# Attention scores and the prompt's scores over all 128 rows of the matmul array, with zeros in the unused half

## The chip, the cores and the metric

One core of one Trainium2 chip. The metric is the device time of one launch in microseconds (us), the median of several runs. All inputs, weights and results are float32.

## What is computed

One inference step of a two-layer trunk over 640 tokens of 1024 features: 128 prompt tokens and 512 latent tokens. Each layer has a Fourier mixer beside differential attention (8 heads, two key maps of 64 features per head), sigmoid gates, an output projection and a gated feed-forward with a short convolution. The part that the change touches is the attention; latent queries see 128 cached keys and the 512 latent ones, prompt queries see the prompt only:

```python
def diff_attention(q, k, v, lam):
    ...
    scale = QK_DIM ** -0.5
    qb = jnp.moveaxis(q.reshape(b, nb, Q_BLOCK, N_HEADS, 2, QK_DIM), 1, 0)
    def one_block(qblk):
        s = jnp.einsum('bqhmd,bkhmd->bhmqk', qblk, k).astype(jnp.float32) * scale
        p = jax.nn.softmax(s, axis=-1)
        pd = p[:, :, 0] - lam * p[:, :, 1]
        return jnp.einsum('bhqk,bkhd->bqhd', pd.astype(v.dtype), v)
```

Here `m` runs over the two maps, `d` over the 64 features of one map, and a block is 128 queries.

## The kernel before

Activations lie transposed, features in partitions and the 640 tokens in columns, in 53 equal buffers of 640 columns ("slots") that are handed out in the order in which they were given back (`alloc`, `give`). A float32 operand that wants accuracy is split into a high part in the type float32r, which the array multiplies in one pass, and a low part, the rest, in the same type; a product is then high x high plus the two mixed ones. Every matmul of the program is issued in `mm` (L265), every transpose in `tr` (L268), so the profile shows these two lines for all of TensorE (PE), and rows are told apart by their tiles: `ps_d`, `ps_s` and `ps_t` are the accumulators (two buffers, one, one). Each matmul has a weight load of its own, in rows marked PEld.

Weights come as blocks of 1 MB into `w_raw` by DMAs that SP issues, are split into `w_h` (ACT L309, or POOL L311 outside attention) and `w_l` (DVE L315), and are used by the projections (`proj`, six matmuls of 320 columns per 128 features).

In attention the heads follow one another. `unit` makes four closures for a block of 128 queries: S0 and S1 (the scores of map 0 and map 1, each followed by its softmax), T (transposes of the combined probabilities), V (the product with the values). `layer` issues S0 of a block, a piece of projection work for the next head, T of the block before, a piece, S1, a piece, V of the block before, a piece. `FILL` sets how long the pieces are. The scheduler of the framework then orders each engine's queue. Per head there are four blocks of latent queries and one of the prompt, so 128 score maps of latent queries in the two layers.

A map of scores is computed in `s_map`. The queries' tile `S[m]` (from `q_epi`) holds the high part of map m's queries in that map's 64 partitions and the low part in the other 64. `KD[m]` (from `k_epi`) holds the high part of the keys in both halves, so that one matmul over 128 rows gives high x high plus low x high. The low part of the keys lies in `KL`, one tile for both maps, map 0 in partitions 0 to 63 and map 1 in 64 to 127; it is multiplied over 64 rows. For each of the two chunks of 320 keys:

```python
self.mm(out=o, lhsT=q, rhs=kd[:, ks], start=True, stop=False)
self.mm(out=o, lhsT=q[a:b], rhs=kl[a:b, ks], start=False, stop=True)
```

DVE then takes the maximum (L629), ACT the exponential (L631), and DVE combines the two maps (L640 to L643). The single `ps_s` is free for the next map when the exponential has read it. After V, ACT squares (L700), POOL makes the norm (L701, L702), DVE scales (L703), and the next T can reuse `ps_t`.

The prompt's scores are float32 products without a split: `qkp` holds its queries in columns 0 to 127 (L554) and its keys in 128 to 255 (L528), and each map takes 64 rows of it.

At the start of a layer the norm's output is made in `hn_one`: ACT L497, POOL L498 and DVE L499 for each of eight feature tiles, and the first projections take them one by one.

## Time and profile before

| what | value |
|---|---|
| runs | 2325.26, 2326.72, 2329.28 us, median 2326.72 |
| profiled execution | span 2324.8 us from the first to the last instruction; the page states no other time for it |
| PE | 2282.7 us busy, 98% of the span |
| weight loads (PEld) | 2122.7 us, 91% |
| DVE, ACT, POOL | 53%, 34%, 15% |
| granted TensorE clock, mean | 0.991 |

Engines are PE (TensorE's matmuls), PEld (its weight loads, which run beside the matmuls), DVE, ACT, POOL, and SP, which issues the DMAs. Matmuls are pipelined and their ends are modelled, so the start times of the weight loads are the better measure of how fast PE steps along. A bracket at the end of a row gives the idle time before it and what ended it; "issue" there means that the engine waited for nothing that the profile shows.

### The profile page before, as it was taken

To read this page: it belongs to the slowest core of one execution; us is meant where nothing else is said; L and a number is where in the kernel's file an instruction comes from. 1 tells how busy PE (TensorE), PEld (TensorE's weight loads), DVE (VectorE), ACT (ScalarE), POOL (GpSimd) and SP (SyncE) were. 2 spreads that over 40 slices of the span, in tenths; PEclk is the share of its full clock that TensorE was granted. 3 is DMA by queue.
4 is the path that set the end of the run, shared out by engine and by line. 5 is a ranking of instruction groups with operands and counts; after the bars stand their busy time and mean duration, and the time that the engine had idled before them with its cause. 6 is when DMAs were issued, how large, how long until landed. Compare 5 with 4: busy or idle time off the path is not lost.

```text
span 2324.8 us, 36711 instructions
## 1 busy us (share of the span) xinstructions
PE 2282.7 (98%) x15142; PEld 2122.7 (91%) x15142; DVE 1227.7 (53%) x2258; ACT 799.5 (34%) x1585; POOL 353.5 (15%) x550
## 2 busy tenths in 40 slices
PE   8999999999999999999999999999999999999998
PEld 5888888999999999999988888789999999999998
DVE  5665665324556553545466655752254565445454
ACT  4555554222133221313245555532122333122231
POOL 2111111101022000010051111210010410000001
PEclk8999999999999999999999999999999999999999
DMA  8222222222212332122212222222222122221221
GB/s 301 81 81 78 81 76 73 109 91 78 87 45 101 146 126 74 60 87 73 73 64 97 79 79 80 74 76 109 91 74 73 55 73 79 85 69 60 91 73 46
DMA packets 40631, 200.41 MB, mean 86 GB/s; under 512 B 4496, under 2 KB 12048, under 8 KB 19344
## 3 DMA queue, kind: packets, MB, share of 16 engines
q1 hardware_dynamic: 40464, 198.07, 24.5%
q8 instruction: 119, 1.95, 0.3%
q14 instruction: 48, 0.39, 0.1%
HBM read 193.33 MB, written 4.72 MB: 85 GB/s over the span
## 4 chain that ended last, share of the span: by engine, by line
PE 84%; issue 6%; DVE 4%; POOL 4%; ACT 2%; DMA 1%; POOLq 0%; SPq 0%; DVEq 0%; ACTq 0%
PE ps_d L265 48%; PE ps_s L265 19%; PE ps_t L265 15%; PE ps_t L268 2%; POOL slot L498 2%; POOL w_h L311 1%; ACT slot L497 1%; ACT slot L631 1%; POOL slot L515 0%; POOL ors L702 0%; ACT slot L534 0%; DVE slot L513 0%; DVE w_l L315 0%; PE ps_d L268 0%; DVE nm L629 0%
## 5 line engine op out<-in xcount | busy, mean ns | idle before, releaser
L265 PE MATMUL ps_d<-slot,w_h 128*128 128x320 f32 x5056 | 1000.0, 315 | 13.5 <-DVE slot L499 12.4
L265 PEld LDWEIGHTS ps_d<-slot,w_h 128*128 128x128 f32 x5056 | 796.0, 189 | 47.1 <-DVE slot L499 19.3
L265 PE MATMUL ps_d<-slot,w_l 128*128 128x320 f32 x2528 | 598.7, 311 | 2.6 <-DVE w_l L315 2.6
L315 DVE TENSOR_TENSOR w_l<-w_raw,w_h 128x512 fp32r<-128x512 f32 x520 | 362.6, 707 | 272.1 <-ACT w_h L309 158.5
L265 PEld LDWEIGHTS ps_d<-slot,w_l 128*128 128x128 f32 x2528 | 429.9, 189 | 3.4 <-DVE w_l L315 2.9
L309 ACT CAST w_h<-w_raw 128x512 fp32r<-128x512 f32 x308 | 188.4, 620 | 472.3 <-PE ps_d L265 244.3
L311 POOL TENSOR_SCALAR w_h<-w_raw 128x512 fp32r<-128x512 f32 x212 | 146.7, 693 | 1222.7 <-PE ps_d L265 622.2
L265 PE MATMUL ps_s<-slot,w_h 128*128 128x320 f32 x1376 | 264.8, 310 | 0.0
L265 PE MATMUL ps_t<-slot,w_h 128*128 128x320 f32 x1376 | 264.5, 309 | 0.0
L265 PEld LDWEIGHTS ps_t<-slot,w_h 128*128 128x128 f32 x1376 | 218.0, 188 | 1.7 <-issue 1.7
L265 PEld LDWEIGHTS ps_s<-slot,w_h 128*128 128x128 f32 x1376 | 217.8, 188 | 1.7 <-ACT slot L937 1.7
L631 ACT ACTIVATE slot<-ps_s,nm 128x640 f32<-128x640 f32 (+1 forms) x160 | 113.6, 710 | 187.1 <-DVE nm L629 184.0
L265 PE MATMUL ps_s<-slot,slot 128*128 128x320 f32 (+1 forms) x512 | 173.8, 392 | 0.9 <-ACT slot L631 0.2
L629 DVE TENSOR_REDUCE nm<-ps_s 128x1 f32<-128x640 f32 (+1 forms) x160 | 114.5, 716 | 104.2 <-PE ps_s L265 96.7
L265 PEld LDWEIGHTS ps_s<-slot,slot 128*128 128x128 f32 (+1 forms) x512 | 94.6, 185 | 78.7 <-issue 64.1
L265 PE MATMUL ps_t<-slot,w_l 128*128 128x320 f32 x688 | 164.6, 309 | 0.0
L265 PE MATMUL ps_s<-slot,w_l 128*128 128x320 f32 x688 | 164.6, 309 | 0.0
L932 DVE SCALAR_TENSOR_TENSOR slot<-ps_d,c_vecs,slot 128x511 f32<-128x511 f32 (+1 forms) x176 | 84.9, 543 | 64.5 <-ACT slot L937 64.5
L265 PEld LDWEIGHTS ps_s<-slot,w_l 128*128 128x128 f32 x688 | 117.1, 188 | 0.0
L265 PEld LDWEIGHTS ps_t<-slot,w_l 128*128 128x128 f32 x688 | 117.1, 188 | 0.0
L265 PE MATMUL ps_d<-w_h,slot 128*128 128x256 f32 x480 | 101.8, 293 | 0.6 <-DVE cols L427 0.6
L701 POOL TENSOR_SCALAR oms<-oss 128x1 f32<-128x1 f32 x80 | 24.7, 309 | 449.4 <-ACT junk L700 421.0
(164 smaller groups left out, 2254.2 us busy)
## 6 DMA issues: line engine op xcount, KB each, us to landing
w_raw<-in_w_stream SPq DMA_DIRECT2D x164, 1024.0 KB, 4.9
slot<-in_w_first SPq DMA_DIRECT2D x32, 256.0 KB, 5.6
w_raw<-in_w_stream SPq DMA_DIRECT2D x8, 768.0 KB, 4.3
slot<-in_x_t SPq DMA_DIRECT2D x8, 320.0 KB, 5.9
out_y_t<-slot SPq DMA_DIRECT2D x8, 320.0 KB, 2.2
c_big<-in_t_big SPq DMA_DIRECT2D x1, 1280.0 KB, 8.4
slot<-in_k_t SPq DMA_DIRECT2D x16, 64.0 KB, 1.8
slot<-in_v_h SPq DMA_DIRECT2D x16, 64.0 KB, 1.8
```

Source lines behind the costliest of these rows:

```text
L265: return self.nc.tensor.matmul(**a)
L268: return self.nc.tensor.transpose(*a)
L309: nc.scalar.copy(out=h[:, a:b], in_=raw[:, a:b])
L311: nc.gpsimd.tensor_scalar(out=h[:, a:b], in0=raw[:, a:b], scalar1=1.0, scalar2=0.0, op0=ALU.mult, op1=ALU.add)
L315: nc.vector.tensor_sub(out=lo[:, a:b], in0=raw[:, a:b], in1=h[:, a:b].bitcast(F32))
L497: nc.scalar.activation(out=H[:, a:b], in_=tmp[:, a:b], func=AF.Identity, scale=A, bias=B)
L498: (eng or nc.gpsimd).tensor_scalar(out=tmp[:, a:b], in0=tmp[:, a:b], scalar1=A, scalar2=B, op0=ALU.mult, op1=ALU.add)
L629: nc.vector.tensor_reduce(out=st["nm"][:, m:m + 1], in_=s_ap, axis=AX.X, op=ALU.max, negate=True)
L631: nc.scalar.activation(out=p[:, 0:n], in_=s_ap, func=AF.Exp, bias=st["nm"][:, m:m + 1], scale=1.0, accum_out=st["sum"][:, m:m + 1])
L701: nc.gpsimd.tensor_scalar(out=ms, in0=ss, scalar1=1.0 / 128, scalar2=EPS, op0=ALU.mult, op1=ALU.add)
L932: nc.vector.scalar_tensor_tensor(out=y[:, o0:o1], in0=ps[:, 192 + i0:192 + i1], scalar=w, in1=y[:, o0:o1], op0=ALU.mult, op1=ALU.add)
```

## The change

The low parts of the keys get a tile per map. `half_tiles` allocates two pairs of slots at the start of each layer (heads use them in turn) and clears the half that is never written; the pairs are given back when the layer's attention is over. The second matmul of each chunk then takes all 128 rows of the queries' tile and of the low keys, the other map's rows being multiplied by zeros. The prompt's queries go into one of two new constant tiles `pq`, map 0 in partitions 0 to 63 of its first 128 columns and map 1 in 64 to 127 of the second 128, with zeros elsewhere; it takes two ACT instructions in place of one, and the prompt's matmuls take 128 rows of it against the whole key tile `kp`. A setting of the launch makes room for the new tiles. The rest of the diff removes comments.

```diff
         self.gsub = [mk(f"c_gsub{l}", [128, 1]) for l in range(DEPTH)]
+        self.pq = [mk(f"c_pq{i}", [128, 256]) for i in range(2)]
...
-        hd = self.head[h] = dict(S=[self.alloc(F32R) for _ in range(2)], KD=[self.alloc(F32R) for _ in range(2)], KL=self.alloc(F32R),
-                                 pr=self.mid("qkp", 256))
+        hd = self.head[h] = dict(S=[self.alloc(F32R) for _ in range(2)], KD=[self.alloc(F32R) for _ in range(2)], KL=self.kl[h % 2],
+                                 pr=self.mid("kp"), pq=self.pq[h % 2])
...
-            nc.scalar.copy(out=hd["pr"][:, 128:256], in_=ps[:, 192:320])
-            nc.sync.dma_start(out=self.O["state_kt"][l, h], in_=hd["pr"][:, 128:256])
+            nc.scalar.copy(out=hd["pr"], in_=ps[:, 192:320])
+            nc.sync.dma_start(out=self.O["state_kt"][l, h], in_=hd["pr"])
...
-            nc.vector.tensor_sub(out=KL[a:b], in0=kr[a:b], in1=KD[m][a:b].bitcast(F32))
+            nc.vector.tensor_sub(out=KL[m][a:b], in0=kr[a:b], in1=KD[m][a:b].bitcast(F32))
...
-            nc.scalar.activation(out=qp[:, 0:128], in_=ps[:, 192:320], func=AF.Copy, scale=0.125)
+            for m, (a, b) in enumerate(((0, 64), (64, 128))):
+                nc.scalar.activation(out=pq[a:b, 128 * m:128 * m + 128], in_=ps[a:b, 192:320], func=AF.Copy, scale=0.125)
...
-            kd, kl = hd["KD"][m], hd["KL"]
-            a, b = (0, 64) if m == 0 else (64, 128)
+            kd, kl = hd["KD"][m], hd["KL"][m]
...
-                self.mm(out=o, lhsT=q[a:b], rhs=kl[a:b, ks], start=False, stop=True)
+                self.mm(out=o, lhsT=q, rhs=kl[:, ks], start=False, stop=True)
...
-                    self.mm(out=s[:, 512 * m:512 * m + 128], lhsT=hd["pr"][a:b, 0:128], rhs=hd["pr"][a:b, 128:256])
+                    self.mm(out=s[:, 512 * m:512 * m + 128], lhsT=hd["pq"][:, 128 * m:128 * m + 128], rhs=hd["pr"])
...
-                self.give(*hd["S"], *hd["KD"], hd["KL"])
+                self.give(*hd["S"], *hd["KD"])
...
         nc.gpsimd.memset(self.cs, 0.0)
+        for t in self.pq:
+            nc.gpsimd.memset(t, 0.0)
...
+    def half_tiles(self):
+
+        self.kl = [[self.alloc(F32R) for _ in range(2)] for _ in range(2)]
+        for pair in self.kl:
+            self.nc.gpsimd.memset(pair[0][64:128].bitcast(F32), 0.0)
+            self.nc.gpsimd.memset(pair[1][0:64].bitcast(F32), 0.0)
...
         self.head, self.v = {}, {}
+        self.half_tiles()
...
         self.in_attn = self.heads_on = False
+        for pair in self.kl:
+            self.give(*pair)
...
-    nc = _bacc.Bacc("TRN2", target_bir_lowering=False, num_devices=1)
+    nc = _bacc.Bacc("TRN2", target_bir_lowering=False, num_devices=1, dynamic_dma_scratch_size=4096)
```

Two places where queues change. POOL at the start of layer 1, before (L498 is the norm's output, the two `c_` names its scale and shift columns, L311 a piece of a weight block, L467 the norm's root):

```order
L467 TENSOR_TENSOR rs<-ms,c_mh 128x3
L311 TENSOR_SCALAR w_h_91<-w_raw_89 128x512 x2
L498 TENSOR_SCALAR slot_10759<-slot_10759,c_a_83,c_mods_80 128x128
L498 TENSOR_SCALAR slot_10759<-slot_10759,c_a_83,c_mods_80 128x192
L498 TENSOR_SCALAR slot_10769<-slot_10769,c_a_83,c_mods_80 128x128
L498 TENSOR_SCALAR slot_10769<-slot_10769,c_a_83,c_mods_80 128x192
L498 TENSOR_SCALAR slot_10776<-slot_10776,c_a_83,c_mods_80 128x128
L498 TENSOR_SCALAR slot_10776<-slot_10776,c_a_83,c_mods_80 128x192
```

The same place with the change (line numbers are one higher there):

```order
L468 TENSOR_TENSOR rs<-ms,c_mh 128x3
L1234 MEMSET slot_10899 64x640
L312 TENSOR_SCALAR w_h_93<-w_raw_91 128x512 x2
L499 TENSOR_SCALAR slot_10771<-slot_10771,c_a_83,c_mods_80 128x128
L499 TENSOR_SCALAR slot_10771<-slot_10771,c_a_83,c_mods_80 128x192
L499 TENSOR_SCALAR slot_10781<-slot_10781,c_a_83,c_mods_80 128x128
L499 TENSOR_SCALAR slot_10781<-slot_10781,c_a_83,c_mods_80 128x192
L1235 MEMSET slot_10900 64x640
L499 TENSOR_SCALAR slot_10788<-slot_10788,c_a_83,c_mods_80 128x128
L499 TENSOR_SCALAR slot_10788<-slot_10788,c_a_83,c_mods_80 128x192
L1234 MEMSET slot_10901 64x640
```

Four memsets come in: one ahead of the weight pieces, the other three (the last stands two rows further on) between the feature tiles of the norm.

ACT in head 0 of layer 0, where the prompt's queries of the next head are written, before (L631 is an exponential, L686 the copy of the transposed probabilities, L559 the high part of the latent queries):

```order
L631 ACTIVATE slot_964,sum<-ps_s,nm 128x640
L554 ACTIVATE qkp<-ps_d 128x128
L686 COPY slot_1002<-ps_t 128x640
L711 ACTIVATE slot_721<-ps_t,c_gsub_87 128x128
L559 ACTIVATE slot_824<-slot_949 64x512
```

and with the change:

```order
L633 ACTIVATE slot_975,sum<-ps_s,nm 128x640
L556 ACTIVATE c_pq_90<-ps_d 64x128 x2
L686 COPY slot_1013<-ps_t 128x640
L711 ACTIVATE slot_733<-ps_t,c_gsub_87 128x128
L561 ACTIVATE slot_836<-slot_960 64x512
```

Two instructions of half the partitions stand where one stood. PE's queue holds the same number of matmuls in both programs.

## Rows read from the trace of the kernel before

**Rows 1.** The page, busy time of each engine over the span.
```profile
PE 2282.7 (98%) x15142; PEld 2122.7 (91%) x15142; DVE 1227.7 (53%) x2258; ACT 799.5 (34%) x1585; POOL 353.5 (15%) x550
```

**Rows 2.** Busy time by stretch, the attention of both layers (stretch: length, engines, PEclk, DMA).
```profile
75.00:410.00 335.00, 332.58 (x2115) 275.12 (x2114) 208.03 (x402) 178.66 (x438) 56.88 (x101) 1.00 0.22 78
...
1219.00:1555.00 336.00, 333.38 (x2119) 275.65 (x2118) 208.06 (x403) 179.26 (x441) 57.09 (x102) 1.00 0.23 78
```

**Rows 3.** Timeline of one query block, all engines: start us, duration us, instruction.
```profile
135.28 0.19 PEld L265 LDWEIGHTS ps_s<-slot,slot 128*128 128x128 f32 x1
...
135.66 0.18 PEld L265 LDWEIGHTS ps_s<-slot,slot 64*128 64x128 f32 x1 [0.19 <-issue]
135.99 0.19 PEld L265 LDWEIGHTS ps_s<-slot,slot 128*128 128x128 f32 x1 [0.15 <-issue]
136.21 0.41 DVE L703 TENSOR_SCALAR on<-ps_t,r,ors 128x128 f32<-128x128 f32 x1 [1.37 <-POOL ors L702]
136.34 0.18 PEld L265 LDWEIGHTS ps_s<-slot,slot 64*128 64x128 f32 x1 [0.16 <-issue]
136.67 0.59 PEld L265 LDWEIGHTS ps_d<-slot,w_h 128*128 128x128 f32 x4 [0.15 <-issue]
...
136.78 0.82 DVE L629 TENSOR_REDUCE nm<-ps_s 128x1 f32<-128x640 f32 x1 [0.16 <-PE ps_s L265]
137.22 0.34 PEld L265 LDWEIGHTS ps_d<-slot,w_l 128*128 128x128 f32 x2
...
137.52 0.62 PEld L268 LDWEIGHTS ps_t<-c_small,slot 128*128 128x128 f32 x5
137.64 0.80 ACT L631 ACTIVATE slot<-ps_s,nm 128x640 f32<-128x640 f32 x1 [2.36 <-DVE nm L629]
...
139.06 0.19 PEld L265 LDWEIGHTS ps_s<-slot,slot 128*128 128x128 f32 x1
...
145.30 0.41 DVE L703 TENSOR_SCALAR on<-ps_t,r,ors 128x128 f32<-128x128 f32 x1 [0.74 <-POOL ors L702]
...
146.44 0.61 PEld L268 LDWEIGHTS ps_t<-c_small,slot 128*128 128x128 f32 x5
```

**Rows 4.** Waits of the weight loads, whole program: total us, times, longest us.
```profile
PEld ps_s L265 <- issue: 65.1, 391, 0.8
...
PEld ps_s L265 <- ACT slot L631: 7.7, 13, 0.8
PEld ps_s L265 <- ACT w_h L309: 6.7, 8, 0.8
...
PEld ps_s L265 <- ACT qkp L554: 2.5, 6, 0.8
```

**Rows 5.** Timeline of the weight loads at a prompt block, layer 1.
```profile
1256.18 0.19 PEld L265 LDWEIGHTS ps_d<-w_h,slot 128*128 128x128 f32 x1
1256.50 0.30 PEld L265 LDWEIGHTS ps_s<-qkp 64*128 64x128 f32 x4
1256.92 0.19 PEld L265 LDWEIGHTS ps_d<-w_h,slot 128*128 128x128 f32 x1
```

**Rows 6.** The tile of the prompt's queries and keys: durations in ns (min/median/max).
```profile
L554 ACT ACTIVATE qkp<-ps_d x16: 266/278/288, 67.1 to 1504.7; 128x128 f32<-128x128 f32 x16
```

**Rows 7.** Timelines of POOL and of the loads: program start, then layer 1's start.
```profile
0.71 0.31 POOL L1080 MEMSET c_cond<- 128x256 f32 x1 [0.29 <-POOLq L1376]
...
5.01 0.32 ACT L1104 ACTIVATE c_cond<-c_vecs 128x8 f32<-128x8 f32 x2
...
1171.33 8.35 POOL L498 TENSOR_SCALAR slot<-slot,c_a,c_mods 128x128 f32<-128x128 f32 x11 [0.15 <-ACT slot L497]
...
1181.77 0.19 PEld L265 LDWEIGHTS ps_d<-slot,w_h 128*128 128x128 f32 x1 [1.83 <-DVE slot L499]
```

**Rows 8.** Busy time between one score map and the next, a head of layer 1.
```profile
1313.90:1318.60 4.70, 4.70 (x31) 4.04 (x30) 3.59 (x6) 4.61 (x8) 0.98 (x2) 1.00 0.05 14
...
1324.10:1328.50 4.40, 4.12 (x26) 3.25 (x27) 4.12 (x10) 1.91 (x5) 1.28 (x1) 1.00 0.67 238
```

More of the change, by code (lines that the diff above doesn't have):

```diff
@@ L548, in q_epi @@
         nc = self.nc
-        S, qp = self.head[h]["S"], self.head[h]["pr"]
+        S, pq = self.head[h]["S"], self.head[h]["pq"]
         qr, tmp = self.alloc(), self.alloc()
@@ L662, in S0 @@
                 for m in range(2):
-                    a, b = (0, 64) if m == 0 else (64, 128)
-                    self.mm(out=s[:, 512 * m:512 * m + 128], lhsT=hd["pr"][a:b, 0:128], rhs=hd["pr"][a:b, 128:256])
+                    self.mm(out=s[:, 512 * m:512 * m + 128], lhsT=hd["pq"][:, 128 * m:128 * m + 128], rhs=hd["pr"])
                 for m in range(2):
```

## The prediction

> **What bounds the kernel now.** I read the page first: PE is busy for 98% of the span, DVE for 53% [rows 1]. So a change pays by what it takes out of PE's queue, as long as the other engines keep up. Then the busy time by stretch, since the change touches attention alone: the two attention stages last 335 and 336 us, and in them DVE is busy for 208 us, 62%, ACT for 179 us, 53% [rows 2]. Their clock is granted in full (1.00, the 2.4 GHz level), so nothing here is a matter of the clock. Third, the timeline of one query block. The reader is to see the starts of the weight loads there [rows 3]: in a projection six loads start in 0.85 us (136.67 to 137.52), 0.142 us each, one running into the next although each lasts some 0.19 us. In a score map the four loads, alternately of 128 and 64 rows, start 0.34 to 0.38 us apart, and so does the projection's first load behind the last of them. Each of these four steps has an idle gap of 0.15 to 0.19 us that ends on "issue": no data was waited for. A score map thus holds PE from 135.28 to 136.67, 1.39 us. Last, the waits of the loads over the whole program: 65.1 us of such gaps ahead of loads for `ps_s`, 391 times, beside which the real waits of the scores for ACT, 7.7 and 6.7 us, are small [rows 4].
>
> So PE steps slower whenever the number of rows changes between 64 and 128, and the score maps do that four times each. The change takes the 64-row form away; with it, I expect the loads to run at the projection's pace.
>
> **The change part by part.**
>
> *Score maps.* Four loads at 0.142 us are 0.57 us; 1.39 less 0.57 is 0.82 us per map. 128 maps give 105.0 us, all on PE's path. The bounds: at least the idle gaps go, 0.19 + 0.15 + 0.16 + 0.15 = 0.65 us per map [rows 3], 83 us; at the most the 105, since no load of that width in the projections starts closer to the next. A bound of nothing is a rival below. I take 105, because the matmuls become the projection's form: 128 rows, 320 columns, the same two types of operand.
>
> The Trainium skill has a rule that speaks against this. "TensorE: Matmul & The Clock Gate", Part 3, "The mechanism", says that a weight load overlaps a running matmul only when it goes to another row group. By it, loads of the full array would not overlap, the score maps would stay at 1.39 us and the sum would hold no gain. The projection's rows disagree: loads that use all rows start 0.142 us apart, less than one lasts.
>
> *Prompt.* Here a normal load starts at 1256.18, the first 64-row load at 1256.50, and 0.42 us later, after four of the prompt's, the next normal one [rows 5]. The step into the 64-row form, 0.32 us, would be 0.142: 0.18 us, times 16 is 2.8 us gained. The bounds: 0.5 us if all five steps come to 0.142 (0.74 less 0.71, times 16), 3.4 if all go at the 0.105 us that the four have among themselves (0.32 less 0.105). Against it, the prompt's queries take two ACT instructions in place of one. The nearest row is the one of 278 ns for 128 partitions [rows 6]; I take the same for 64, so 0.28 us more. Six times the prompt's loads waited for that write, 2.5 us in all [rows 4]: 6 x 0.28 = 1.7 us lost, at the most 16 x 0.28 = 4.5, at the least nothing. The other ten hide behind projection work that stands ahead of the block in PE's queue.
>
> *Clearing the halves.* A memset of 256 columns on POOL took 0.31 us [rows 7]; by columns 640 take 0.78 us. At the start four of them stand ahead of the one for `c_cond`, 3.1 us: it then ends at about 0.71 + 3.1 + 0.31 = 4.1 us. ACT needs it at 5.01 [rows 7], so that costs nothing; if that cover were gone, it would cost up to 3.1 us. The two for `pq` follow and end at 4.8. At the start of layer 1 three of the four stand between the feature tiles of the norm. POOL runs there without a break from 1171.33 on, and PE waits at the end of that chain, 1.83 us in the row at 1181.77 [rows 7]. So 3 x 0.78 = 2.3 us go straight to the end; the first memset stands ahead of weight pieces and has room. Each of the three also waits for a DVE reader of its slot, at the most one DVE instruction each, some 0.5 us: 2.3 to 4 us.
>
> *Slots, DMAs, the low part's subtraction.* The subtraction writes another tile, with the same columns: nothing. No DMA is added; SP's queue keeps its transfers. Two more slots are held through attention; the slot that a block's new tile takes was then given back more recently. I cost it at nothing: each was read by PE or DVE half a block earlier, by work that stands ahead anyway. If that cover is gone it is a rival.
>
> *What is late next.* Three kinds of work wait between PE's pieces. Within a block, map 1 waits for the exponential of map 0: maximum at 136.78, exponential from 137.64 to 138.44, next map at 139.06 [rows 3], 0.62 us to spare. No score map lies between, so the change doesn't shorten that. The transposes wait for the scaling by DVE L703: from 136.62 to 137.52, 0.90 us to spare, and in the next block 145.71 to 146.44, 0.73 [rows 3]. A score map does lie in that stretch, so it shrinks by 0.82 and the second of the two is 0.09 us short; over 64 blocks that is up to 5.8 us. And DVE and ACT run their queues in order. Between two maps ACT was busy for 4.61 of 4.70 us, two maps on DVE for 4.12 of 4.40 [rows 8]; with 0.82 taken off they are 0.73 and 0.54 us short, 1.3 us a head, 20 us over 16 heads if the neighbouring stretches soak up none of it. Together the bounds are nothing and 26 us. I take 15: about as much again as the 14.4 us of waits for ACT that the scores have already [rows 4], and a little over the middle.
>
> *Sum.* -105.0 - 2.8 + 1.7 + 2.3 + 15 = -88.8 us. Against the profiled execution, span 2324.8, that is a span of 2236; the median of the runs is 1.9 us above that span, so **2238 us** for the median. With all bounds at their good ends (-105 - 3.4 + 0 + 2.3 + 0) it is 2221; with the bad ends of everything but the maps (-105 - 0.5 + 4.5 + 4 + 26) 2256; with the gaps alone gone and the middle of the rest (-83 + 1 + 15) 2260.
>
> **The rivals.**
>
> *The softmax becomes the bound.* For: DVE goes from 208 in 335 us to 208 in about 290, 72%, and in single stretches over 100%. Against: on the average there is room, and the tight link, exponential to next map, keeps its slack. If each map gives half of its 0.82 us back, 52 us in place of the 15, the time is 2238 + 37 = 2275.
>
> *The gap is not from the rows.* It could belong to something that stays: a new moving tile at every matmul, or queries that are loaded twice. Then nothing is saved, and the new work on POOL and ACT costs 2 to 4 us: 2330. This is also where the skill's rule above ends; with the projections' rows against it, I give it little. Against the other reading: the projections change their moving tile at every matmul too, without a gap, and in the prompt the loads show the step at the edge to 64 rows (1256.18 to 1256.50) and none among the four [rows 5].
>
> *Slower: slots run short.* With two fewer free slots a new probability tile could have to wait for the transposes of the block before; then the exponential, and with it the next map, starts later in every block, and PE stands. The gain is spent where that costs 1.64 us a block (105 / 64); at 2.2 us a block the result is 2238 + 141 - 15 = 2364. For: the buffers are handed out in order of return. Against: PE has no wait of that kind now, and the exponential starts as soon as the maximum is there (137.60 to 137.64) [rows 3].
>
> **How the numbers follow.** The forecast with its own bounds, 2221 to 2256, has 72%; gaps alone, about 2260, 9%; the softmax as the bound, about 2275, 13%; no gain, 2330, 4%; slots, 2%. The range 2220 to 2266 takes in the first two and the near part of the third, some 84%. A difference of 0.2% (4.7 us) is about what a measurement can tell from no change. Faster takes the first three, 0.94; the case without gain lies on both sides of that line, so 0.03 for the same, and 0.03 for slower.
>
> **What would show it.** In the profile after: score loads all of 128 rows, starting about 0.14 us apart, and the projection's load right behind; the "issue" gaps ahead of `ps_s` down from 65 us to a few; the two attention stages some 290 us each, with everything after them unchanged; DVE's busy time there the same 208 us. Waits of the scores for ACT L631 and of the transposes for DVE L703 in the tens of us would show the 15 too small. PE waiting about 2.3 us longer at layer 1's start would show the memsets. Score loads still 0.34 us apart would make the prediction wrong at its first step.

## The result, and the profile after

| what | before | after |
|---|---|---|
| median of the runs | 2328.0 us (2325.3 to 2330.0) | 2256.5 us (2252.5 to 2259.8) |
| ratio, 95% interval | | 0.9693, 0.9681 to 0.9705 |
| span of the profiled execution | 2324.8 us | 2250.7 us |
| granted TensorE clock, mean | 0.991 | 0.99 |

The change makes the kernel 71.5 us faster. The time lies inside the predicted range (2220 to 2266) and 18.5 us above the predicted 2238. The profile tells which terms held; the profiled execution of the kernel after is the fastest of its four, so its span is 74.1 us shorter where the medians differ by 71.5. Lines of the kernel after are one to two higher than before: matmuls are L266, transposes L269, the maximum L631, the exponential L633; the scaling is still L703.

The page of the kernel after, busy time of each engine (to be held against [rows 1]):

```profile
PE 2190.9 (97%) x15142; PEld 2108.7 (94%) x15142; DVE 1224.7 (54%) x2258; ACT 799.7 (36%) x1601; POOL 365.1 (16%) x560
```

Its two attention stages, busy time by stretch as in [rows 2]:

```profile
73.80:369.00 295.20, 284.58 (x2100) 265.78 (x2099) 203.33 (x392) 177.04 (x443) 59.47 (x98) 1.00 0.26 88
1178.00:1478.00 300.00, 289.26 (x2119) 270.17 (x2118) 203.91 (x394) 179.59 (x447) 59.75 (x99) 0.99 0.26 89
```

From the first load of the prompt's scores to the load behind the last score map the stages lasted 333.8 and 336.6 us before and 295.8 and 300.1 after. They are 38.0 and 36.5 us shorter, 74.5 together, and the whole span is 74.1 us shorter: next to nothing happened anywhere else. But PE was busy 333 us of 335 before, and now some 285 of 295 and 289 of 300. It has begun to wait. The waits of the weight loads over the whole program, as in [rows 4] (total us, times, longest):

```profile
PEld ps_s L266 <- ACT slot L633: 19.3, 29, 2.1
...
PEld ps_s L266 <- ACT w_h L310: 8.4, 10, 0.8
PEld ps_t L269 <- DVE on L703: 5.2, 6, 1.1
...
PEld ps_s L266 <- ACT c_pq L556: 2.4, 6, 0.8
...
PEld ps_s L266 <- issue: 0.8, 4, 0.2
```

The 65 us of "issue" gaps ahead of `ps_s` are down to 0.8. The waits of the scores for the exponential rose from 7.7 us in 13 waits to 19.3 in 29. One place in the timeline of the kernel after shows both (start us, duration us, instruction, the idle time before it):

```profile
134.99 0.63 PEld L266 LDWEIGHTS ps_s<-slot,slot 128*128 128x128 f32 x4
...
135.58 0.63 PEld L266 LDWEIGHTS ps_d<-slot,w_h 128*128 128x128 f32 x4
135.67 0.37 ACT L700 ACTIVATE junk<-ps_t,r 128x128 f32<-128x128 f32 x1
...
136.49 0.54 POOL L702 TENSOR_TENSOR ors<-oms,c_mh 128x1 f32<-128x1 f32 x1
...
137.07 0.41 DVE L703 TENSOR_SCALAR on<-ps_t,r,ors 128x128 f32<-128x128 f32 x1 [0.74 <-POOL ors L702]
137.51 0.82 DVE L540 TENSOR_TENSOR slot<-slot,slot 64x640 fp32r<-64x640 f32 x1
137.53 0.53 PEld L269 LDWEIGHTS ps_t<-c_small,slot 128*128 128x128 f32 x5 [1.03 <-DVE on L703]
...
138.36 0.82 DVE L631 TENSOR_REDUCE nm<-ps_s 128x1 f32<-128x640 f32 x1
139.22 0.79 ACT L633 ACTIVATE slot<-ps_s,nm 128x640 f32<-128x640 f32 x1 [1.18 <-DVE nm L631]
140.16 0.59 PEld L266 LDWEIGHTS ps_s<-slot,slot 128*128 128x128 f32 x4 [1.14 <-ACT slot L633]
```

The reader is to see two things. The map's four loads, all of 128 rows, hold PE from 134.99 to 135.58: 0.59 us where it was 1.39 [rows 3]. And nothing uses the map for the next 2.5 us: its maximum starts only at 138.36, although its matmuls are done by about 135.9. Ahead of the maximum in DVE's queue stands the scaling L703 of the block before, which waits for the square on ACT (L700) and two small operations on POOL (the second one is the row of L702), and behind L703 the low part of a head's keys (L540). So the maximum is late, the exponential is late, map 1 waits 1.14 us, and the transposes wait 1.03 us for the same L703. Before, the maximum stood behind L703 too. In that kernel, two maps earlier than the one above, at 136.78, it still waited 0.16 us for the map [rows 3]: there the old map was just as long as that chain over POOL. The same map as the one above starts at 144.18 in the kernel before, with L703 at 145.30 [rows 3]:

```profile
144.18 0.19 PEld L265 LDWEIGHTS ps_s<-slot,slot 128*128 128x128 f32 x1
...
146.60 0.82 DVE L629 TENSOR_REDUCE nm<-ps_s 128x1 f32<-128x640 f32 x1
...
148.39 0.19 PEld L265 LDWEIGHTS ps_s<-slot,slot 128*128 128x128 f32 x1 [0.38 <-ACT slot L631]
```

Here the maximum started 2.42 us behind the map's first load, where it is 3.37 us after, and map 1 waited 0.38 us where it now waits 1.14. Over all 64 first maps of a block, the maximum started on average 1.66 us behind the map's first load before and 1.74 us after, although the map itself is 0.80 us shorter. The maximum did not move up with the map. DVE's waits for POOL at L703 did not grow either (63.9 us before, 52.5 after, in the waits of DVE).

**Where the 74 us come from.** For every weight load from the first score map of a layer to the end of its last one I took the time to the next load's start, less a wait for another engine named there, and summed by tile, both layers together:

| loads | before | after | difference |
|---|---|---|---|
| score maps, 128 of them | 176.2 us | 73.4 us | -102.9 |
| projections (`w_h`, `w_l` against a slot) | 235.1 us | 241.4 us | +6.3 |
| prompt's scores | 5.9 us | 6.6 us | +0.7 |
| all other loads | 213.0 us | 212.6 us | -0.4 |
| waits for another engine | 30.9 us | 52.9 us | +22.0 |
| together | 661.1 us | 586.8 us | -74.3 |

The waits in this table are not all waits for data. In either kernel, 24 times in the two stages, the load behind eight small loads of `c_cond` (the product of raw weights with the conditions) stands still for at least 0.84 us, and the profile names one engine or another for it. PE's own row shows it computing all that time (its ends are modelled; but in the kernel with the scaling cut in two, below, all 24 stops last 0.84 us, whichever engine is named). Here is one in the kernel after:

```profile
90.71 0.16 PEld L266 LDWEIGHTS ps_d<-w_raw,c_cond 128*32 128x32 f32 x8 [0.20 <-issue]
90.71 1.07 PE L266 MATMUL ps_d<-w_raw,c_cond 128*32 128x512 f32 x8
...
91.70 0.59 PEld L266 LDWEIGHTS ps_s<-slot,slot 128*128 128x128 f32 x4 [0.84 <-ACT w_h L310]
```

Without 0.84 us for each such stop the waits are 12.4 us before and 32.7 after, 20.3 more: the score maps' loads wait 16.0 us in place of 2.6 and the transposes 10.1 in place of 3.3. Below I call these the waits without the fixed stops.

Part of the 6 us of the projections is a loss of something that the gap had given: four loads directly behind a map took 0.55 us (136.67 to 137.22 in [rows 3]); now they take 0.59 us, like four loads behind other loads of a projection.

### The profile page after: what moved, and what is told of

Its sections match the earlier page's. It is cut to its first block, busy times and chain, and to the rows that moved or that the text cites. A ratio compares the mean times of both kernels' runs of the same rounds, so it can differ in the third digit from the quotient of the medians.

```text
span 2250.7 us, 36749 instructions
## 1 busy us (share of the span) xinstructions
PE 2190.9 (97%) x15142; PEld 2108.7 (94%) x15142; DVE 1224.7 (54%) x2258; ACT 799.7 (36%) x1601; POOL 365.1 (16%) x560
## 4 chain that ended last, share of the span: by engine, by line
PE 75%; issue 8%; DVE 5%; ACT 5%; POOL 5%; DMA 2%; SPq 0%; POOLq 0%; ACTq 0%; DVEq 0%
PE ps_d L266 44%; PE ps_t L266 15%; PE ps_s L266 15%; POOL slot L499 2%; POOL ors L702 1%; ACT slot L633 1%; PE ps_t L269 1%; DVE nm L631 1%; ACT slot L535 1%; DMA slot<-in_w_first 1%; ACT junk L700 1%; DVE slot L514 1%; POOL oms L701 1%; ACT slot L536 1%; DMA w_raw<-in_w_stream 1%
## 5 line engine op out<-in xcount | busy, mean ns | idle before, releaser
L266 PE MATMUL ps_d<-slot,w_h 128*128 128x320 f32 x5056 | 989.3, 313 | 14.8 <-DVE slot L500 13.8
L266 PEld LDWEIGHTS ps_d<-slot,w_h 128*128 128x128 f32 x5056 | 799.6, 189 | 32.6 <-DVE slot L500 19.9
L266 PE MATMUL ps_d<-slot,w_l 128*128 128x320 f32 x2528 | 598.1, 311 | 2.6 <-DVE w_l L316 2.6
L316 DVE TENSOR_TENSOR w_l<-w_raw,w_h 128x512 fp32r<-128x512 f32 x520 | 361.9, 706 | 266.8 <-ACT w_h L310 156.5
L266 PEld LDWEIGHTS ps_d<-slot,w_l 128*128 128x128 f32 x2528 | 430.6, 189 | 2.9 <-DVE w_l L316 2.9
L266 PE MATMUL ps_s<-slot,w_h 128*128 128x320 f32 x1376 | 264.8, 310 | 0.0
L266 PE MATMUL ps_t<-slot,w_h 128*128 128x320 f32 x1376 | 264.4, 309 | 0.0
L266 PEld LDWEIGHTS ps_t<-slot,w_h 128*128 128x128 f32 x1376 | 218.1, 188 | 1.7 <-issue 1.7
L266 PEld LDWEIGHTS ps_s<-slot,w_h 128*128 128x128 f32 x1376 | 217.9, 188 | 1.7 <-ACT slot L937 1.7
L633 ACT ACTIVATE slot<-ps_s,nm 128x640 f32<-128x640 f32 (+1 forms) x160 | 113.6, 710 | 152.7 <-DVE nm L631 151.1
L266 PE MATMUL ps_t<-slot,w_l 128*128 128x320 f32 x688 | 164.6, 309 | 0.0
L266 PE MATMUL ps_s<-slot,w_l 128*128 128x320 f32 x688 | 164.6, 309 | 0.0
L631 DVE TENSOR_REDUCE nm<-ps_s 128x1 f32<-128x640 f32 (+1 forms) x160 | 113.9, 712 | 57.7 <-PE ps_s L266 50.4
L266 PEld LDWEIGHTS ps_s<-slot,w_l 128*128 128x128 f32 x688 | 117.2, 188 | 0.0
L266 PEld LDWEIGHTS ps_t<-slot,w_l 128*128 128x128 f32 x688 | 117.2, 188 | 0.0
L266 PE MATMUL ps_s<-slot,slot 128*128 128x320 f32 x512 | 101.5, 320 | 10.5 <-ACT slot L633 10.5
L266 PEld LDWEIGHTS ps_s<-slot,slot 128*128 128x128 f32 x512 | 77.5, 188 | 30.6 <-ACT slot L633 19.3
L266 PE MATMUL ps_d<-w_h,slot 128*128 128x256 f32 x480 | 99.5, 288 | 0.6 <-DVE cols L428 0.6
L932 DVE SCALAR_TENSOR_TENSOR slot<-ps_s,c_vecs,slot 128x511 f32<-128x511 f32 x88 | 42.6, 543 | 89.1 <-ACT slot L937 89.1
```

What stands on the lines that cost most here:

```text
L266: return self.nc.tensor.matmul(**a)
L316: nc.vector.tensor_sub(out=lo[:, a:b], in0=raw[:, a:b], in1=h[:, a:b].bitcast(F32))
L631: nc.vector.tensor_reduce(out=st["nm"][:, m:m + 1], in_=s_ap, axis=AX.X, op=ALU.max, negate=True)
L633: nc.scalar.activation(out=p[:, 0:n], in_=s_ap, func=AF.Exp, bias=st["nm"][:, m:m + 1], scale=1.0, accum_out=st["sum"][:, m:m + 1])
L932: nc.vector.scalar_tensor_tensor(out=y[:, o0:o1], in0=ps[:, 192 + i0:192 + i1], scalar=w, in1=y[:, o0:o1], op0=ALU.mult, op1=ALU.add)
```

## Experiments

Twelve kernels. Ratios are against the kernel before on the same chip (medians 2326.8 to 2329.4 us), with 95% intervals.

### Which part of the change carries the gain

**The order of the products alone.** The kernel before, with its 64-row products kept, but both products of a kind together:

```diff
-            for c in range(2):
-                o = s[:, PSO[c]:PSO[c] + 320]
-                ks = slice(320 * c, 320 * c + 320)
-                self.mm(out=o, lhsT=q, rhs=kd[:, ks], start=True, stop=False)
-                self.mm(out=o, lhsT=q[a:b], rhs=kl[a:b, ks], start=False, stop=True)
+            for low in range(2):
+                for c in range(2):
+                    o = s[:, PSO[c]:PSO[c] + 320]
+                    ks = slice(320 * c, 320 * c + 320)
+                    if low:
+                        self.mm(out=o, lhsT=q[a:b], rhs=kl[a:b, ks], start=False, stop=True)
+                    else:
+                        self.mm(out=o, lhsT=q, rhs=kd[:, ks], start=True, stop=False)
```

> The kernel before with one thing changed: a score map issues its two products over 128 rows first and then its two over 64 rows, so that the number of rows changes twice per map and not four times. Theory A (each change between 64 and 128 rows costs PE some 0.2 us): 0.41 us less per map, 52 us over 128 maps, less 5 to 15 us of new waits for the softmax: 2280 to 2290 us, and no gap between the two loads of 64 rows. Rival B (a matmul over 64 rows is slow by itself, wherever it stands): the loads of 64 rows stay 0.34 us from their neighbours and the time stays at 2327.

Measured: 2286.5 us, ratio 0.9817 (0.9797 to 0.9838). The timeline of the weight loads at one map of this kernel:

```profile
129.96 0.34 PEld L265 LDWEIGHTS ps_s<-slot,slot 128*128 128x128 f32 x2
130.48 0.29 PEld L265 LDWEIGHTS ps_s<-slot,slot 64*128 64x128 f32 x2 [0.18 <-issue]
130.97 0.59 PEld L265 LDWEIGHTS ps_d<-slot,w_h 128*128 128x128 f32 x4 [0.19 <-issue]
```

There are two gaps, one at each change of the number of rows, and none between the two loads of 64 rows. Over 128 maps, a map held PE for 0.99 us on average, between the 1.38 of before and the 0.57 of the change. So the price lies in the change of rows, not in the 64-row load itself, nor in a new moving tile at every matmul, which the maps of the change still have. Reordering, which costs no buffers, brings 41 us of the 71.5.

**The tiles without the products.** The kernel before with the two held pairs of low keys, their memsets and the changed setting of the launch; the products still take 64 rows of them, and the prompt is as before.

```diff
-KL=self.alloc(F32R),
+KL=self.kl[h % 2],
...
+        self.half_tiles()
...
-            kd, kl = hd["KD"][m], hd["KL"]
+            kd, kl = hd["KD"][m], hd["KL"][m]
```

> The kernel before with the two pairs of low-key tiles held through each layer's attention and their halves cleared, but the matmuls still over 64 rows and the prompt as before. Theory A: the tiles and their memsets cost little, 2326 to 2331 us. Rival C (two slots fewer make the softmax wait, which is where the 15 us of missing gain went): 10 us or more slower than before, 2337 or above.

Measured: 2328.6 us, ratio 1.0002 (0.9993 to 1.0012). The memsets and the two slots cost nothing that can be measured; the interval runs from 1.6 us faster to 2.8 us slower.

**The change without the prompt's part.** Latent scores as in the change, the prompt's products on 64 rows of `qkp` as before.

```diff
-            for m, (a, b) in enumerate(((0, 64), (64, 128))):
-                nc.scalar.activation(out=pq[a:b, 128 * m:128 * m + 128], in_=ps[a:b, 192:320], func=AF.Copy, scale=0.125)
+            nc.scalar.activation(out=qp[:, 0:128], in_=ps[:, 192:320], func=AF.Copy, scale=0.125)
...
-                    self.mm(out=s[:, 512 * m:512 * m + 128], lhsT=hd["pq"][:, 128 * m:128 * m + 128], rhs=hd["pr"])
+                    self.mm(out=s[:, 512 * m:512 * m + 128], lhsT=hd["pr"][a:b, 0:128], rhs=hd["pr"][a:b, 128:256])
```

> The change without its prompt part: the prompt's queries and keys share one tile and are multiplied over 64 rows, as before. Theory A: the prompt's part gains under 3 us and its extra ACT instruction costs about as much, so 2254 to 2260 us. Rival D (the extra ACT and POOL work of the prompt's part takes the missing gain): 2240 to 2248.

Measured: 2255.5 us, ratio 0.9695 (0.968 to 0.9709), against 0.9693 for the whole change. The prompt's part is worth nothing that can be measured, either way.

**Two more slots.** The change with `NSLOT = 55` in place of 53.

> The changed kernel with 55 slots in place of 53, so that attention has as many free slots as before the change. Theory A (the missing gain is lost to DVE and ACT running their queues in order): no difference, 2252 to 2260 us. Rival C (slots run short): 15 us or so come back, 2238 to 2245.

Measured: 2253.2 us, ratio 0.9681 (0.9666 to 0.9695); the scores wait 20.7 us for the exponential, 29 times. The new waits are not for buffers.

### What the new waits are

**Projection work dealt out otherwise.** The change with

```diff
-FILL = (1.3, .5, 1.1, 1.1)
+FILL = (1.8, .5, .8, .9)
```

The four pieces stand behind S0, T, S1 and V in turn. The expectation names the first two places wrongly: 45% stands between map 0 and the transposes, and 12.5% between the transposes and map 1.

> The changed kernel, with the projection work dealt out otherwise between PE's four steps of a block: 45% of it (before 32.5%) between map 0 and map 1, 12.5% as before between map 1 and the transposes' step behind it, and less in the other two places. Nothing else changes. Theory A (about 31 us of what the score maps saved went into new waits of PE: map 1 for the exponential of map 0, which has now less projection work beside it, and the transposes for DVE): the waits of the score loads for ACT's exponential, 19 us with 29 waits in the changed kernel, fall to about 8 us, and if the transposes' waits don't grow by as much the time is 2240 to 2252. Theory B (DVE and ACT are too slow on the whole between two blocks, wherever the projection work stands): the waits only move, from map 1 to map 0 or to the transposes, and the time stays at 2253 to 2260.

Measured: 2263.1 us, ratio 0.9717 (0.9702 to 0.9733), 6.6 us above the change (5.6 by the two ratios). The waits of the weight loads:

```profile
PEld ps_s L266 <- ACT slot L633: 25.3, 39, 1.3
...
PEld ps_t L269 <- DVE w_l L316: 6.7, 8, 0.8
```

Told apart by the step before them, the waits at map 1 fell from 22.0 to 11.6 us, and those at map 0 rose from 7.4 to 20.4. (The eight waits of the transposes for L316 are fixed stops.) Without the fixed stops, map 1 went from 15.3 to 11.6 us, map 0 from 0.7 to 13.7, and all waits from 32.7 to 40.1. The waits moved, as theory B said, and grew; more cover at one place takes it from the next.

**Half of the low weight parts on POOL**, while attention runs:

```diff
-                nc.vector.tensor_sub(out=lo[:, a:b], in0=raw[:, a:b], in1=h[:, a:b].bitcast(F32))
+                eng = nc.gpsimd if self.heads_on and (a // 512) % 2 else nc.vector
+                eng.tensor_tensor(out=lo[:, a:b], in0=raw[:, a:b], in1=h[:, a:b].bitcast(F32), op=ALU.subtract)
```

> The changed kernel, with every second subtraction that makes a low part of weights moved from DVE to POOL while attention runs; the numbers computed are the same. It relieves DVE by about 10 to 15 us per attention stage. Theory A1 (the new waits come from DVE's queue: the maxima, the scaling and the combining stand behind low parts of weights): the transposes' waits for DVE fall by half, and the time is 2243 to 2252. Theory A2 (they come from ACT's queue, the exponential above all): no change within 4 us of 2256. Rival: POOL is slower at it and its small operations of the softmax come later; then the transposes wait more and the time is 2258 to 2275.

Measured: 2266.0 us, ratio 0.9733 (0.9716 to 0.9749). A group of instructions of this kernel (busy us, mean ns, idle time before):

```profile
L317 POOL TENSOR_TENSOR w_l<-w_raw,w_h 128x512 fp32r<-128x512 f32 x48 | 65.7, 1370 | 75.3 <-ACT w_h L310 75.2
```

A piece takes 1370 ns on POOL and 706 on DVE. DVE's busy time in the two stages fell from 203 and 204 to 196 and 194 us, and the scores wait 27.5 us for the exponential, not less.

**Half of the high weight parts on POOL**, while attention runs:

```diff
-                if self.heads_on or self.hcount % 2:
+                if self.hcount % 2:
```

> The changed kernel, with every second rounding that makes a high part of weights moved from ACT to POOL while attention runs, as the kernel does outside of attention. It relieves ACT by about 20 us or more per attention stage. Theory A2 (the exponential comes late because ACT's queue is full of high parts of weights): the waits of the score loads for the exponential, 19 us, fall by half and the time is 2240 to 2250. Theory A1 (DVE's queue): no change within 4 us of 2256. Rival: POOL's small operations of the softmax stand behind the roundings, the transposes wait more, 2260 to 2280.

Measured: 2261.2 us, ratio 0.9712 (0.9698 to 0.9726). ACT is relieved of 12 us per stage (177 and 180 to 165 and 167), and the scores wait 25.8 us for the exponential. In both runs the rival came true: with less work on DVE or on ACT the waits did not get shorter. That speaks against the sum of an engine's work, but does not settle it, since both edits also put longer pieces into POOL's queue ahead of the small operations of the softmax. The next edit leaves that out.

**The scaling cut in two.** If an instruction at the head of DVE's queue makes them, it is L703, which waits for POOL while the maximum stands behind it. The edit lets DVE do its half without POOL's result:

```diff
-            nc.vector.tensor_scalar(out=on, in0=o, scalar1=st["r"][:, 0:1], scalar2=rs, op0=ALU.mult, op1=ALU.mult)
+            nc.vector.tensor_scalar(out=on, in0=o, scalar1=st["r"][:, 0:1], scalar2=1.0, op0=ALU.mult, op1=ALU.mult)
+            nc.gpsimd.tensor_scalar(out=on, in0=on, scalar1=rs, scalar2=1.0, op0=ALU.mult, op1=ALU.mult)
```

On the change:

> The changed kernel with DVE's scaling of a block's result cut in two: DVE multiplies by the first factor straight out of PSUM as soon as the product with the values is there, and POOL multiplies by the second factor, which it has just computed, in place. DVE then waits for no POOL result at the head of its queue, and ps_t is free before POOL is done. Theory A, in its narrower form (the chain product, square on ACT, two small operations on POOL, scaling on DVE stands ahead of the next map's maximum in DVE's in-order queue; the old score map was long enough to hide it, the new one is not): DVE's waits for POOL's result ahead of the scaling, 54 us in the changed kernel, are gone, the transposes' waits for the scaling (5 us by name) too, the score loads' waits for the exponential fall from 19 us to some 8, and the time is 2230 to 2247. Theory B (the waits are the sum of DVE's and ACT's work, no matter which instruction waits at the head): within 4 us of 2256. Rival: POOL's longer chain makes the result's own transpose late; 2258 to 2270.

On the kernel before:

> The kernel before, with the same cut of the scaling into a DVE and a POOL instruction. Theory A in its narrower form: DVE waited there for POOL as well (64 us), but the score map of 1.39 us covered it; so the time falls by less than 8 us, to 2319 to 2328, and the gain of the change on top of this edit is larger than on its own, 80 us or more in place of 71.5. Theory B: no change, 2325 to 2331, and the change is worth the same 71.5 us on top of it. If the edit pays here as much as in the changed kernel, the wait had cost all along and is no part of what the change lost.

Measured: on the change 2233.6 us, ratio 0.9602 (0.9582 to 0.9621); on the kernel before 2321.3 us, ratio 0.9975 (0.9965 to 0.9984). The same edit is worth 5.5 us before and 22.9 us after (21 by the two ratios), and on top of it the change is worth 87.7 us in place of 71.5. The edit takes out POOL's part and no more: from the start of the square on ACT to that of the scaling on DVE it is 0.75 us, on average of 80 blocks, where it was 1.73, while the square follows the end of the product with the values by 0.29 us where it was 0.31. The timeline of the change with the cut, at the same place as above:

```profile
134.28 0.63 PEld L266 LDWEIGHTS ps_s<-slot,slot 128*128 128x128 f32 x4
...
135.37 0.34 DVE L703 TENSOR_SCALAR on<-ps_t,r 128x128 f32<-128x128 f32 x1
...
135.74 0.82 DVE L540 TENSOR_TENSOR slot<-slot,slot 64x640 fp32r<-64x640 f32 x1
135.77 0.59 PEld L269 LDWEIGHTS ps_t<-c_small,slot 128*128 128x128 f32 x5
...
136.27 0.54 POOL L704 TENSOR_SCALAR on<-on,ors 128x128 f32<-128x128 f32 x1
136.60 0.82 DVE L631 TENSOR_REDUCE nm<-ps_s 128x1 f32<-128x640 f32 x1
136.86 0.14 PEld L269 LDWEIGHTS ps_t<-c_small,on 128*128 128x128 f32 x1 [0.50 <-POOL on L704]
...
138.39 0.60 PEld L266 LDWEIGHTS ps_s<-slot,slot 128*128 128x128 f32 x4 [0.59 <-ACT slot L633]
```

From the map's first load to the scaling it is 1.09 us where it was 2.08, to the transposes 1.49 where it was 2.54, to the maximum 2.32 where it was 3.37, and map 1 waits 0.59 us instead of 1.14. The waits of its loads over the program:

```profile
PEld ps_s L266 <- ACT slot L633: 11.6, 21, 1.1
...
PEld ps_t L269 <- POOL on L704: 5.8, 10, 1.0
```

The load waits between the first and last maps, counted as in the table above, are 28.6 us in place of 52.9, and 13.5 in place of 32.7 without the fixed stops; the kernel before had 12.4. Of these 19.2 us, 8.2 went at the score maps and 7.5 at the transposes; the edit does not tell apart what the earlier maximum and what the earlier release of `ps_t` brought, since it moves both. Over the 64 first maps of a block the maximum now starts 1.19 us behind the map's first load, on average, in place of 1.74. On the kernel before, the edit took the waits without the fixed stops from 12.4 to 4.2 us. With 2233.6 us this kernel is faster than both the one before and the change.

**The scaling left whole, behind the maximum.** In program order only; the framework's scheduler still orders the queue.

```diff
+        if kind == "t":
+            self.scale()
...
             nc.vector.tensor_reduce(out=st["nm"][:, m:m + 1], in_=s_ap, axis=AX.X, op=ALU.max, negate=True)
+            self.scale()
...
-            nc.vector.tensor_scalar(out=on, in0=o, scalar1=st["r"][:, 0:1], scalar2=rs, op0=ALU.mult, op1=ALU.mult)
+            self.late = lambda: nc.vector.tensor_scalar(out=on, in0=o, scalar1=st["r"][:, 0:1], scalar2=rs, op0=ALU.mult, op1=ALU.mult)
...
+    def scale(self):
+        f, self.late = self.late, None
+        f and f()
```

> The changed kernel with the scaling left whole, but put behind the next map's maximum in DVE's queue instead of ahead of it. Theory A in its narrower form: the maximum, and with it the exponential and map 1, come earlier, the score loads' waits for the exponential fall from 19 us to about 8; but ps_t is set free later by up to a maximum's 0.8 us, so the transposes wait more. The two are of about the same size: 2245 to 2265, with the waits moved from the scores to the transposes. Theory B: 2253 to 2260 with the waits as they were.

Measured: 2252.1 us, ratio 0.9682 (0.9659 to 0.9705). The waits of the scores for the exponential are 19.6 us, as they were. The run decides nothing: in DVE's rows only 14 of the 80 scalings stand directly behind a maximum; in the block shown above the old order stayed. The scheduler undid most of the edit.

### What is left after the cut

**A shorter maximum.** The cut kernel, with the maximum over 128 of a map's 640 columns:

```diff
-            nc.vector.tensor_reduce(out=st["nm"][:, m:m + 1], in_=s_ap, axis=AX.X, op=ALU.max, negate=True)
+            nc.vector.tensor_reduce(out=st["nm"][:, m:m + 1], in_=s_ap[:, 0:128], axis=AX.X, op=ALU.max, negate=True)
```

> The kernel with the scaling cut in two, and the maximum of a score map taken over 128 of its 640 columns instead of all; the maximum only shifts the exponents, so what is computed is otherwise the same. It takes some 0.5 us out of the chain from one map to the next and 60 us of busy time off DVE, and nothing off PE. What is left of waits in attention after the cut is some 32 us. Theory A (what is left is again the chain map, maximum, exponential, next map): the score loads' waits for the exponential, 11.6 us, go to under 4 and the time falls to 2205 to 2222. Rival (what is left belongs to ACT's queue, the high parts of weights and the copies): the time stays within 5 us of 2233.6.

Measured: 2239.1 us, ratio 0.9619 (0.9603 to 0.9635). Its maxima as a group of instructions, and its loads' waits:

```profile
L631 DVE TENSOR_REDUCE nm<-ps_s 128x1 f32<-128x128 f32 x160 | 45.8, 287 | 89.6 <-PE ps_s L266 82.5 <-ACT slot L633 5.9
```

```profile
PEld ps_s L266 <- ACT slot L633: 8.6, 13, 0.9
PEld ps_t L269 <- POOL on L704: 8.3, 15, 1.2
```

A maximum takes 287 ns in place of 714, and the kernel did not get faster: 5.4 us more by the medians, 4.0 by the two ratios, whose intervals overlap. The waits for the exponential fell by 3 us, but without the fixed stops they are 8.6 us where they were 8.3, and all waits are 18.5 where they were 13.5. What is left of waits does not hang on the length of the maximum: theory A fails here.

**A shift of the projection work on top of the cut:** `FILL = (1.45, .5, .95, 1.1)`.

> The kernel with the scaling cut in two, and a little more of the projection work ahead of the transposes (36% in place of 32.5%) and less between map 1 and the product with the values (24% in place of 27.5%). Theory A: with the transposes waiting little now, there is room to shift; map 1 waits less for the exponential of map 0, map 0 not much more for that of map 1, and the time is 2225 to 2232. Rival: as in the first shift of this kind the waits only move, or grow, and the time is 2233 to 2242.

Measured: 2241.7 us, ratio 0.9623 (0.9609 to 0.9638). As in the first shift the waits moved: without the fixed stops, at map 1 from 6.1 to 4.5 us, at map 0 from 1.7 to 9.2, and at the transposes from 2.6 to 2.8; together they are 18.8 in place of 13.5.

## Why the prediction was right, and which terms were off

**The score maps: right.** Forecast 105.0 us (1.39 to 0.57 us a map), measured 102.9 (1.38 to 0.57 on average; the old steps are 0.33 to 0.38 us in [rows 3], where the prediction has 0.34). The loads start about 0.15 us apart (134.99 to 135.58 for four), the gaps are gone, and DVE's busy time in a stage is 203 us, nearly what it was. The rule of the Trainium skill that the prediction weighed ("TensorE: Matmul & The Clock Gate", Part 3, "The mechanism": a load overlaps a running matmul only in another row group), taken alone, would have left the map at its old length; these loads of all 128 rows, each lasting 0.19 us, overlap all the same, and the trace decides. The same section of the Trainium skill also lets the engine pull ahead loads into a background weight buffer, so it does not rule the overlap out; no run here shows where a load goes.

**Gaps alone, no gain: fallen.** The first would have left some 22 us in the maps; the second is answered by the grouped kernel, whose gaps sit exactly at the changes of rows, and by the change itself, whose maps keep their moving tiles and have no gap.

**The prompt: off, small.** The forecast was -2.8 + 1.7 us. Its loads in attention take 0.7 us more, not less, and the scores wait for the queries 2.4 us in 6 waits, as before (2.5 in 6), so the second ACT instruction was hidden everywhere. The kernel without this part ran the same.

**The memsets: too dear.** Forecast 2.3 us. The kernel with the tiles alone shows no difference, but its interval of 0.9993 to 1.0012 would still hold 2.3 us; the trace says more. At layer 1's start the loads wait 6.1 us for the norm's DVE instructions where they waited 5.6 (from the waits of the loads in that stretch of either kernel). The memsets took 0.63 us on POOL each, not 0.78, and PE's wait at the end of that chain grew by 0.5 us only.

**What is late next: the term that failed.** The prediction put 15 us there, with a bound of 26. Load waits between the maps rose by 22.0 us, or 20.3 without the fixed stops, inside the bound. The 15 was in part a matter of luck: it was set by the 14.4 us of waits for ACT that the scores had already [rows 4], and 14 of those 21 waits, all eight for L309 and six of the thirteen for L631, were fixed stops; only 2.6 us were waits. The prediction named the right places (map 1 behind the exponential, the transposes behind L703), but it reasoned that the exponential's chain keeps its slack because "no score map lies between" maximum and next map. It measured that slack from the maximum's old start, and the maximum did not move up with the map: it stands behind L703 and other work in DVE's queue, and L703 waits for POOL. At 136.78 in [rows 3] the maximum had waited 0.16 us for the map; of the 0.82 us by which the map became shorter, the maximum could use 0.16 there. On average it starts as late behind the map's first load as it did (1.74 us, before 1.66). The cut of the scaling shows the cause by taking it away: 19.2 us of waits go and 22.9 us of time, while the same cut is worth 5.5 us before.

**The rest: not in the sum.** The projections' loads take 6.3 us more. The prediction had nothing for that. The faster start of four loads behind the old map explains about 3 of it: 84 such groups took 0.551 us on average and take 0.585. With the scaling cut in two the projections take 239.2 us, so another 2 of it went with the waits; for the last us I have no cause.

**Slots: fallen.** Two more slots left the waits where they were. **The softmax as the bound** came true in part: PE gives back 20 to 22 of 103 us, but mostly to one instruction's wait, as the cut of the scaling shows, and not to the amount of work; the two runs that relieve DVE and ACT agree with that without settling it.

**Open.** After the cut 13.5 us of load waits remain beside the fixed stops, much as the 12.4 in the kernel before. Neither a shorter maximum nor another deal of projection work removes them. The fixed stops themselves, some 20 us, stand in all these kernels; no run tried to shorten them. Since each edit also lets the scheduler order the queues anew, differences of 5 us between such variants may come from that alone, and these runs do not tell it apart.

## What to carry to other kernels

Look at the starts of the weight loads, not at the busy share: gaps that end on "issue" between loads of different row counts are a price of the switch, and putting equal shapes next to each other already takes half of it away, without buffers. When a step on the bounding engine becomes shorter, ask for each consumer of its result what it last waited for: one that waited 0.16 us for the step can use 0.16 us of the gain. And an instruction that waits for a third engine at the head of an in-order queue holds up all that stands behind it; it can be worth cutting it into the part that can run now and the part that has to wait. Before a wait is put down to the engine that the profile names, look whether the waiting engine's own work fills that time: here 12 of the 14.4 us that looked like waits for ACT were PE computing.

## What was not expected of the hardware

Four switches of the row count cost 0.80 us a map and two cost 0.41 (0.986 less 0.573), so 0.20 each, and two loads of 64 rows behind each other show no gap at all. A subtraction of 512 columns on POOL takes 1370 ns and on DVE 706. And POOL's power operation on 128 x 1 values, the same instruction in both kernels, went from 625 to 727 ns on average when attention became denser (50.0 to 58.2 us in 80 instructions), as the groups of instructions of before and after show:

```profile
L702 POOL TENSOR_TENSOR ors<-oms,c_mh 128x1 f32<-128x1 f32 x80 | 50.0, 625 | 6.8 <-POOL oms L701 0.2
```

```profile
L702 POOL TENSOR_TENSOR ors<-oms,c_mh 128x1 f32<-128x1 f32 x80 | 58.2, 727 | 6.7
```

The median stayed, at 542 and 543 ns. 13 of the 80 took over 0.6 us before and 29 after, up to 1.14 us. In the timelines every one of these ran while DVE was at work on an instruction with two large inputs (L643 before; L645 after, and L732 twice), and none that ran beside an idle DVE took longer than 0.59 us. No run tried this by itself.
